# Norm factors put on behind the projections, and half of a recurrence's operands made on another engine

## The chip, the cores and the metric

The kernel runs on one core of a Trainium2 chip. The metric is the device time of one execution in microseconds; before the change the median of three runs is 1512.39 us (1511.13 to 1512.42). A profile of one execution, with every instruction's start and duration, is the basis of all that follows. TensorE (PE) multiplies, VectorE (DVE), ScalarE (ACT) and GpSimd (POOL) work elementwise, and SyncE (SP) issues most of the transfers.

## The reference

Two transformer blocks are computed for 256 tokens of 1024 features in float32. The change touches only the mixer of the first block, which is, cut to what matters:

```python
u = rmsnorm(h, norm1_g)        # h * rsqrt(mean(h*h) + 1e-6) * g, the mean over the features of a token
proj = u @ w_in
p_rwkv, p_att, p_idx, p_gate = split(proj)
y_a = rwkv7_mix(token_shift(p_rwkv, tshift_mu), ...)
q, k = rope(q), rope(k)                      # q, k, v from p_att
y_b = dsa_attention(q, k, v, rope(q_idx), rope(k_idx), w_idx)
g_a, g_b = split(sigmoid(p_gate))
h = h + (g_a * (y_a @ w_o_rwkv) + g_b * (y_b @ w_o_att)) @ w_out
```

`token_shift(p, mu)` is `p + (prev - p) * mu` with `prev` the token before. `rwkv7_mix` is a recurrence over time with a 64 by 64 state per head, decays, and normalised keys. The norm's factor belongs to a token, so it can be put on `u` or on any column of `proj`. Behind the mixer come a gated feed-forward layer, and the second block with its own mixer and a mixture of 64 experts; these are as they were.

## The kernel before

**Layout.** Features lie on partitions, tokens along the free axis: the input `xT` is eight blocks of 128 features by 256 tokens. A projection group is 256 columns of a weight matrix, loaded as one tile `w` of 128 by 2048 (L258), so two slots `w0`, `w1` hold two groups.

**Three products for one.** Each operand is split in a high part (rounded) and a low part (the rest): `wh` by a cast on ScalarE (L272), `wl` by a subtraction on VectorE (L273), in pieces of 128 by 512. These are kept in a ring of three half groups. The activation has `uh` and `ul` in the same way. `dense` (L299) issues, for eight blocks of features and two halves of the columns, the three products high-high, high-low and low-high: 48 products of 128x256 per group. The weight pieces are the product's first operand, so the output has columns on partitions, and a token's factor lies along the free axis.

**The norm.** `Rms` squares the input on ScalarE (L375), adds pairs of blocks on VectorE (L382), sums over partitions with TensorE (`nps`, L390), takes the root on ScalarE (L394) and its reciprocal on VectorE (L395), and `rows` (L406) spreads the 256 factors over all partitions with TensorE (`rsp`). Then `scaled_parts` (L427) multiplies each block by gain and factor on VectorE (L433), casts `uh` on ScalarE (L435) and makes `ul` on VectorE (L436). `hold` keeps the first weight casts behind the root in ScalarE's order. `raw_pair` (L420), which multiplies by the gain alone, is used at the second norm.

**What is done with the groups.** First group 6, whose columns are the low-rank inputs of decay, rate and gate (`lor0`). Then for head group 0 its r, k, v (groups 0, 2, 4), and for head group 1 groups 1, 3, 5; `shift_group` (L466) does the token shift out of PSUM, one scaled copy on ScalarE and one multiply-add on VectorE per 128 columns. `rwkv(g)` (L556) makes the decays (`sg`, `aa`, `cum`, `cpv`: sigmoid, running sum, exponentials), normalises the keys (`kk`, by `kps`, a root, a reciprocal of `kn` and the spreading `bps`), and writes the operands of the chunked recurrence: `zr` with minus-kk times decay (L625) and r times decay (L627), `bh` = `aa` and `kh` = `km` divided by the decay, and `bp`, `kp` (L635, L636, GpSimd), which are transposed (`tps`). Products `mps` give masks `MB`, `MK`; `solve` inverts a triangular system in six levels, with masks made on GpSimd (L497); then four steps of the recurrence run. `dsa_proj` (L778) makes the groups of the attention, with a rotation of q, k and the indexer's by `cos` and `sin`; `gate_steps` (L812) takes a group through tanh on ScalarE; `select` keeps 64 keys per query, by eight rounds of MAX and MATCH_REPLACE on VectorE; `attend` follows.

**What sets the order.** Each engine runs its instructions in one fixed order. The framework's scheduler interleaves the code's chains when the kernel is built, and waits are kept by semaphores; so an instruction that waits holds up all behind it on its engine. Projection groups fill TensorE while the recurrence's short products wait on other engines.

## Time and profile before

| | |
|---|---|
| runs, median | 1512.39 us |
| profiled execution, its own time | 1515.65 us |
| its span | 1513.9 us |
| TensorE busy | 1438.2 us, 95% |
| VectorE busy | 823.9 us, 54% |
| ScalarE busy | 596.1 us, 39% |
| GpSimd busy | 137.0 us, 9% |
| DMA | 362.10 MB, mean 239 GB/s |

The first block's mixer, where the change lies, takes about the first 345 us. A profile's timeline row gives the start, the time, the engine, the source line, the operation with output and inputs, the shape and how many were merged; in brackets stands the idle time of the engine before it and who ended it. PEld is TensorE's weight load. Busy shares over the whole span mix stages with different limits, so the windows and timelines of a stage are what to read.

### The profile page before, as it was taken

To read this page: it belongs to the slowest core of one execution; us is meant where nothing else is said; L and a number is where in the kernel's file an instruction comes from. 1 tells how busy PE (TensorE), PEld (TensorE's weight loads), DVE (VectorE), ACT (ScalarE), POOL (GpSimd) and SP (SyncE) were. 2 spreads that over 40 slices of the span, in tenths; PEclk is the share of its full clock that TensorE was granted. 3 is DMA by queue.
4 is the path that set the end of the run, shared out by engine and by line. 5 is a ranking of instruction groups with operands and counts; after the bars stand their busy time and mean duration, and the time that the engine had idled before them with its cause. 6 is when DMAs were issued, how large, how long until landed. Compare 5 with 4: busy or idle time off the path is not lost. (4 is left out here: it accounts for less than half of the span.)

```text
span 1513.9 us, 28057 instructions
## 1 busy us (share of the span) xinstructions
PE 1438.2 (95%) x11310; PEld 1157.3 (76%) x11310; DVE 823.9 (54%) x1664; ACT 596.1 (39%) x1221; POOL 137.0 (9%) x131
## 2 busy tenths in 40 slices
PE   6999999989999989899999999999999999988996
PEld 6788988989999969798898999996554544543543
DVE  4787488577998968855854567653122121211211
ACT  5543356555545467444534555552111111111110
POOL 2143210000100100310230000100000000000000
PEclk9999999989999989899999999999999999999999
DMA  5311244549978345222321433975999999999996
GB/s 197 123 50 42 67 161 140 184 167 422 389 292 306 125 165 186 84 84 72 124 85 56 168 115 109 347 284 197 352 413 421 423 422 421 422 422 422 421 423 264
DMA packets 58627, 362.10 MB, mean 239 GB/s; under 512 B 6912, under 2 KB 7552, under 8 KB 20352
## 3 DMA queue, kind: packets, MB, share of 16 engines
q1 hardware_dynamic: 56912, 357.77, 60.7%
q10 hardware_dynamic: 1584, 2.52, 0.5%
q8 instruction: 90, 1.47, 0.4%
q14 instruction: 41, 0.34, 0.1%
HBM read 357.51 MB, written 1.05 MB: 237 GB/s over the span
## 5 line engine op out<-in xcount | busy, mean ns | idle before, releaser
L286 PE MATMUL dps<-uh,wh 128*128 128x256 f32 x1280 | 376.2, 294 | 4.2 <-ACT wh L272 2.1
L286 PE MATMUL dps<-uh,wl 128*128 128x256 f32 x1280 | 365.0, 285 | 4.0 <-DVE wl L273 4.0
L286 PE MATMUL dps<-ul,wh 128*128 128x256 f32 x1280 | 365.2, 285 | 0.7 <-DVE ul L439 0.5
L286 PEld LDWEIGHTS dps<-uh,wh 128*128 128x128 f32 x1280 | 244.0, 191 | 15.5 <-issue 8.6
L286 PEld LDWEIGHTS dps<-ul,wh 128*128 128x128 f32 x1280 | 243.6, 190 | 7.0 <-issue 4.3
L286 PEld LDWEIGHTS dps<-uh,wl 128*128 128x128 f32 x1280 | 243.4, 190 | 6.2 <-DVE wl L273 4.8
L273 DVE TENSOR_TENSOR wl<-w,wh 128x512 fp32r<-128x512 f32 x267 | 193.1, 746 | 58.0 <-ACT wh L272 56.4
L286 PE MATMUL gup<-wx,xg 128*32 128x512 f32 (+2 forms) x1016 | 201.8, 600 | 20.7 <-DMA wx<-in_w_exp_dram 20.7
L272 ACT CAST wh<-w 128x512 fp32r<-128x512 f32 x267 | 154.4, 615 | 141.8 <-PE dps L286 100.2
L286 PEld LDWEIGHTS gup<-wx,xg 128*32 128x32 f32 (+2 forms) x1016 | 58.6, 122 | 138.4 <-issue 99.5
L273 DVE TENSOR_TENSOR wl<-wm,wh 128x512 fp32r<-128x512 f32 x200 | 140.3, 732 | 39.6 <-ACT wh L272 39.3
L272 ACT CAST wh<-wm 128x512 fp32r<-128x512 f32 x200 | 115.9, 618 | 111.3 <-PE dps L286 72.7
L1694 DVE COPY cs<-pxt 128x1 f32<-128x1 f32 x27 | 4.3, 158 | 216.0 <-PE pxt L289 216.0
L1720 DVE TENSOR_TENSOR yl<-dnp,yh 128x512 fp32r<-128x512 f32 x54 | 37.3, 691 | 153.4 <-ACT yh L1719 153.4
L286 PE MATMUL dnp<-wx,hT 128*32 128x512 f32 (+1 forms) x528 | 100.2, 596 | 2.1 <-DMA wx<-in_w_exp_dram 1.4
L1700 ACT ACTIVATE sgx<-gup 128x256 f32<-128x256 f32 x27 | 10.4, 384 | 222.0 <-PE gup L286 222.0
L1719 ACT CAST yh<-dnp 128x512 fp32r<-128x512 f32 x54 | 31.6, 585 | 119.6 <-PE dnp L286 119.6
L286 PEld LDWEIGHTS dnp<-wx,hT 128*32 128x32 f32 (+1 forms) x528 | 27.9, 120 | 46.3 <-issue 39.5
L996 DVE SCALAR_TENSOR_TENSOR ada<-wm,ct,ada 128x512 f32<-128x512 f32 x76 | 59.5, 825 | 0.0
L286 PE MATMUL acc<-PT,yh 128*128 128x256 f32 x216 | 55.1, 293 | 0.0
L286 PE MATMUL gat<-P,hth 128*128 128x256 f32 (+1 forms) x224 | 54.8, 287 | 0.0
L286 PE MATMUL acc<-PT,yl 128*128 128x256 f32 x216 | 53.0, 283 | 0.6 <-DVE yl L1720 0.6
(541 smaller groups left out, 2795.3 us busy)
## 6 DMA issues: line engine op xcount, KB each, us to landing
wx<-in_w_exp_dram SPq DMA_DIRECT2D x159, 1024.0 KB, 15.9
w<-in_w_in_dram SPq DMA_DIRECT2D x44, 1024.0 KB, 4.9
wm<-in_w_ada_dram SPq DMA_DIRECT2D x22, 1024.0 KB, 7.8
wm<-in_w_in_dram SPq DMA_DIRECT2D x21, 1024.0 KB, 4.9
wh<-in_w_exp_dram SPq DMA_DIRECT2D x33, 512.0 KB, 15.9
wl<-in_w_exp_dram SPq DMA_DIRECT2D x33, 512.0 KB, 14.7
wm<-in_ffn_in_dram SPq DMA_DIRECT2D x16, 1024.0 KB, 9.2
wm<-in_ffn_out_dram SPq DMA_DIRECT2D x7, 1024.0 KB, 9.3
```

The source lines that it names most:

```text
L272: nc.scalar.copy(hi[:, c:e], x[:, c:e])
L273: nc.vector.tensor_sub(lo[:, c:e], x[:, c:e], hi[:, c:e].bitcast(F32))
L286: latest[0] = nc.tensor.matmul(*args, **kw)
L996: nc.vector.scalar_tensor_tensor(y, x, ct[:, k:k + 1], y, op0=ALU.mult, op1=ALU.add)
L1694: nc.vector.tensor_copy(self.cs, px[:, 256:257])
L1700: nc.scalar.activation(sg, self.pg[:, 0:256], AF.Silu)
L1719: nc.scalar.copy(yh[:, quar(c, 512)], pd)
L1720: nc.vector.tensor_tensor(yl[:, quar(c, 512)], pd, yh[:, quar(c, 512)].bitcast(F32), op=ALU.subtract)
```

## The change

The mixer's projections take the input times the gain only. The factors are computed behind the first group's products: `Rms` gets a list `later`, in which the squares are kept, and `factors()` sums them, takes the root, and writes the factors as a column `rsc` per token tile, as rows `rsr`, and scaled as `rsw`. They are then put on in several ways. `times_rs` multiplies a group's sums in PSUM by `rsr`, in place, on VectorE: for the seven shift groups and the eight gate groups, 15 in all. The rotated groups get it by `cos` and `sin`, which are multiplied once on GpSimd. The values and the index weights, whose tokens lie on partitions, get it as the scale of their copy on ScalarE. `hold` goes. The second part: the r-times-decay operands of `zr` (four instructions per head group) are made on GpSimd instead of VectorE. Nothing else is changed in the code.

```diff
+            if self.later is None:
+                self.sums(0, sq[:, 0, :], g)
+            else:
+                self.later.append((sq[:, 0, :], g))
+
+        def finish(self):
+            self.p = pt("d", "nps")
+            for x, g in self.later:
+                self.sums(0, x, g)
...
-                with tc.issue_after(hold[0]) if hold else nullcontext():
-                    nc.scalar.copy(hi[:, c:e], x[:, c:e])
+                nc.scalar.copy(hi[:, c:e], x[:, c:e])
...
-    norm = Rms(xT, r2(0))
+    norm = Rms(xT, r2(0), None, [])
+    uu = parts()
     for g in range(4):
         norm.pair(g)
-    _, uu, _ = scaled_parts(xT, lambda b: pcol("norm1_g", b), norm.rows(norm.columns()))
-    hold.append(norm.root.ins)
+    def factors():
+        norm.finish()
+        rsc.append(norm.columns())
+        nc.vector.tensor_scalar(rsw, rsc[0], float(64 ** -0.5 * 8 ** -0.5), None, op0=ALU.mult)
+        nc.scalar.copy(rsr, norm.rows(rsc[0]))
+
+    def times_rs(p):
+        p3 = p.rearrange("p (a s) -> p a s", a=2)
+        nc.vector.tensor_tensor(p3, p3, rsr.unsqueeze(1).to_broadcast([128, 2, S]), op=ALU.mult)
+        return p
...
         p = yield from dense(A["w_in"][g], uu)
+        if not rsc:
+            factors()
+        times_rs(p)
...
-    whole(shift_group(6, lor0))
-    hold.clear()
+    steps = shift_group(6, lor0)
+    for g in range(4):
+        raw_pair(uu, xT, lambda b: pcol("norm1_g", b), g)
+        for _ in range(2 if g else 0):
+            next(steps)
+    whole(steps)
...
                 load_consts(rp, 1)
+                for t in ("cos", "sin"):
+                    nc.gpsimd.tensor_tensor(cc(t), cc(t), rsr, op=ALU.mult)
...
-                nc.vector.tensor_tensor(zr[hf, j, :, i, 1, :], ck(r)[hf, j], ck(PP)[hf, j], op=ALU.mult)
+                nc.gpsimd.tensor_tensor(zr[hf, j, :, i, 1, :], ck(r)[hf, j], ck(PP)[hf, j], op=ALU.mult)
...
-            nc.scalar.activation(wi[:, n, :], p[:, 0:8], AF.Copy, scale=float(64 ** -0.5 * 8 ** -0.5))
+            nc.scalar.activation(wi[:, n, :], p[:, 0:8], AF.Copy, scale=rsw[:, n:n + 1])
...
-            nc.scalar.copy(vt[:, :, 256 * i:256 * (i + 1)], p.rearrange("p (n c) -> p n c", n=2))
+            for n in range(2):
+                nc.scalar.activation(vt[:, n, 256 * i:256 * (i + 1)], p[:, 256 * n:256 * (n + 1)], AF.Copy, scale=rsc[0][:, n:n + 1])
...
-        nc.scalar.activation(t, (yield from dense(src, uu)), AF.Tanh, scale=0.5)
+        p = yield from dense(src, uu)
+        nc.scalar.activation(t, times_rs(p) if first else p, AF.Tanh, scale=0.5)
```

Since the scheduler places every instruction anew, the order moves on all engines up to the end of the mixer; behind it, it is the same. Three places matter. A row gives line, operation, output and inputs (tile numbers behind the names where they tell rows apart), shape and count.

First, TensorE at the start. Before, its first rows are:

```order
L286 MATMUL nps<-ones,nsq 128x1 x8
L286 MATMUL rsp<-cst_74,rsc 128x128 x2
L286 MATMUL dps<-uh,wh 128x256
L286 MATMUL dps<-ul,wh 128x256
L286 MATMUL dps<-uh,wh 128x256
```

Now the products of group 6 come first, with five of the eight sums between the second and the third of them; behind its last product stand:

```order
L283 MATMUL dps<-uh,wl 128x256
L283 MATMUL dps<-uh,wh 128x256
L283 MATMUL dps<-ul,wh 128x256
L283 MATMUL dps<-uh,wl 128x256
L283 MATMUL nps<-ones,nsq 128x1 x3
L283 MATMUL rsp<-cst_74,rsc 128x128 x2
L283 MATMUL dps<-uh,wh 128x256
L283 MATMUL dps<-ul,wh 128x256
```

The last sums and the broadcast `rsp` moved from before the first product to behind the 48th, ahead of group 0.

Second, VectorE at the key normalisation of head group 0. Before, from the decay to the reciprocal of `kn` (`wl_1075` is the second half of group 3's weights):

```order
L575 TENSOR_TENSOR cpv_471<-cum_470,sg_453 128x512
L627 TENSOR_TENSOR zr_516<-r_229,cum_470 64x4x64 x4
L473 SCALAR_TENSOR_TENSOR r_232<-dps_998,par_72,r_232 128x255
L607 TENSOR_SCALAR km_502<-aa_454,par_72,oka_143 128x256 x2
L273 TENSOR_TENSOR wl_1075<-w_1066,wh_1074 128x512
L597 TENSOR_SCALAR kn_482<-kn_482 8x256
L609 TENSOR_TENSOR km_502<-km_502,k_230 128x512
L598 RECIPROCAL kn_482<-kn_482 8x256
```

Now, for the same stretch (`dps_999` is group 1's sums, and `wl_1077` are the two last pieces of group 3's weights):

```order
L607 TENSOR_TENSOR cpv_472<-cum_471,sg_454 128x512
L476 TENSOR_TENSOR dps_999<-dps_999,rsr_101 128x512
L639 TENSOR_SCALAR km_503<-aa_455,par_72,oka_105 128x256 x2
L270 TENSOR_TENSOR wl_1077<-w_1068,wh_1076 128x512
L641 TENSOR_TENSOR km_503<-km_503,k_226 128x512
L270 TENSOR_TENSOR wl_1077<-w_1068,wh_1076 128x512
L629 TENSOR_SCALAR kn_483<-kn_483 8x256
L645 SCALAR_TENSOR_TENSOR rk_507<-r_225,par_72,km_503 128x256
L630 RECIPROCAL kn_483<-kn_483 8x256
```

The four `zr` rows are gone, a multiplication of group 1's sums stands in their place, and both pieces of `wl_1077` come before the reciprocal, where before only one did.

Third, TensorE at the transposes behind that. Before, 30 products of groups 3 and 5 lie between the transposes of `v` and the first of `bp`; the end of them and the transposes are:

```order
L286 MATMUL dps_1132<-ul_115,wh_1135 128x256
L286 MATMUL dps_1132<-uh_114,wl_1136 128x256
L286 MATMUL dps_1132<-uh_114,wh_1135 128x256
L286 MATMUL dps_1132<-ul_115,wh_1135 128x256
L286 MATMUL dps_1132<-uh_114,wl_1136 128x256
L286 MATMUL dps_1132<-uh_114,wh_1135 128x256
L289 MATMUL tps_546<-cst0_74,bp_530 128x128
L289 MATMUL tps_550<-cst0_74,kp_531 128x128
```

Now, from the transposes of `v` on (`dps_1135` is group 5, `dps_1747` the indexer's narrow group, `lps` the low-rank products of head group 1):

```order
L286 MATMUL tps_542<-cst0_74,v_227 128x128 x2
L283 MATMUL dps_1135<-uh_87,wh_1138 128x256
L283 MATMUL dps_1135<-ul_88,wh_1138 128x256
L283 MATMUL lps_1206<-lor_213,low0_107 128x512
L283 MATMUL lps_1210<-sgd_214,low1_108 128x256
L283 MATMUL dps_1747<-uh_87,wh_1750 72x256
L283 MATMUL dps_1747<-ul_88,wh_1750 72x256
L286 MATMUL tps_547<-cst0_74,bp_531 128x128
L286 MATMUL tps_551<-cst0_74,kp_532 128x128
L286 MATMUL tps_547<-cst0_74,bp_531 128x128
L286 MATMUL tps_551<-cst0_74,kp_532 128x128
```

Group 3's last products moved ahead of the transposes of `v`, and those of group 5 behind the transposes of `bp` and `kp`.

## Rows read from the trace of the kernel before

**Rows 1.** Windows: start:end, length, busy us of PE, PEld, DVE, ACT, POOL; clock, DMA.

```profile
60.00:70.00 10.00, 7.51 (x35) 6.12 (x34) 9.79 (x20) 1.97 (x6) 3.49 (x5) 0.83 0.11 31
...
330.00:340.00 10.00, 6.36 (x44) 6.21 (x43) 5.76 (x12) 6.54 (x12) 0.00 (x0) 0.79 0.45 152
340.00:350.00 10.00, 10.00 (x77) 10.00 (x76) 3.19 (x5) 4.63 (x8) 0.29 (x1) 0.87 1.01 422
...
220.00:250.00 30.00, 28.37 (x218) 25.72 (x217) 29.18 (x98) 17.38 (x43) 0.00 (x0) 1.00 0.27 94
```

**Rows 2.** Timeline of the first 30 us, several engines.

```profile
2.15 0.91 SPq L258 DMA_DIRECT2D w<-in_w_in_dram  x2
...
7.07 0.17 DVE L459 TENSOR_SCALAR omm<-par 128x14 f32<-128x14 f32 x1 [6.05 <-DMA par<-in_params_dram]
...
7.23 1.42 DVE L382 TENSOR_TENSOR nsq<-nsq 128x256 f32<-128x256 f32 x4
...
11.83 1.22 PE L286 MATMUL rsp<-cst,rsc 128*128 128x128 f32 x4 [0.55 <-DVE rsc L395]
...
19.34 0.58 PE L286 MATMUL dps<-uh,wl 128*128 128x256 f32 x1 [1.40 <-DVE wl L273]
...
24.63 0.41 PE L286 MATMUL dps<-uh,wl 128*128 128x256 f32 x1
...
24.84 0.41 PE L286 MATMUL dps<-uh,wh 128*128 128x256 f32 x1
...
25.24 0.28 PE L286 MATMUL dps<-uh,wl 128*128 128x256 f32 x1
...
25.36 0.28 PE L286 MATMUL dps<-uh,wh 128*128 128x256 f32 x1
...
27.68 0.47 ACT L472 ACTIVATE lor<-dps,omm 128x256 f32<-128x256 f32 x1 [2.31 <-PE dps L286]
```

**Rows 3.** Tile w in the first 14 us: from issue to landing.

```profile
DMA to landing us min/median/max: 7.4/8.6/9.9
```

**Rows 4.** Page, costliest groups: ScalarE's weight casts (count, busy, mean ns).

```profile
L272 ACT CAST wh<-w 128x512 fp32r<-128x512 f32 x267 | 154.4, 615 | 141.8 <-PE dps L286 100.2
```

**Rows 5.** Groups by form, VectorE, 0 to 340 us (busy us, mean ns).

```profile
L425 DVE SCALAR_TENSOR_TENSOR ul<-hT,par,uh 128x256 fp32r<-128x256 f32 x8 | 3.5, 480 | 0.6 <-ACT uh L424 0.6
```

**Rows 6.** Groups by form, VectorE, 340 to 560 us.

```profile
L963 DVE TENSOR_TENSOR silu<-dps,rsf 128x512 f32<-128x512 f32 x11 | 7.6, 687 | 3.2 <-PE dps L286 3.2
```

**Rows 7.** Timeline of VectorE, 27 to 112 us.

```profile
54.10 1.53 DVE L627 TENSOR_TENSOR zr<-r,cum 64x256 f32<-64x256 f32 x4 [3.40 <-ACT cum L582]
...
58.12 1.73 DVE L598 RECIPROCAL kn<-kn 8x256 f32<-8x256 f32 x1
...
66.00 0.68 DVE L630 TENSOR_TENSOR aa<-aa,sg 128x512 f32<-128x512 f32 x1
...
82.16 0.68 DVE L504 TENSOR_TENSOR X<-sps,cst 128x512 f32<-128x512 f32 x1
82.75 1.47 DVE L273 TENSOR_TENSOR wl<-w,wh 128x512 fp32r<-128x512 f32 x1
```

**Rows 8.** Timeline of TensorE, 58 to 76 us.

```profile
63.30 0.44 PE L289 MATMUL tps<-cst,v 128*128 128x128 f32 x2
66.14 0.58 PE L286 MATMUL dps<-uh,wl 128*128 128x256 f32 x1 [2.40 <-DVE wl L273]
...
71.31 0.27 PE L289 MATMUL tps<-cst,bp 128*128 128x128 f32 x1
```

**Rows 9.** Timeline of GpSimd, 27 to 112 us.

```profile
66.83 0.92 POOL L635 TENSOR_TENSOR bp<-aa,PC 128x256 f32<-128x256 f32 x1 [4.47 <-DVE aa L630]
...
69.76 1.06 POOL L636 TENSOR_TENSOR kp<-km,PC 128x256 f32<-128x256 f32 x1
...
82.38 1.30 POOL L497 TENSOR_TENSOR nm<-MB,cst 128x512 f32<-128x512 f32 x1 [0.69 <-DVE XT L505]
```

More of the change, by code (lines that the diff above doesn't have):

```diff
@@ L241, in _body @@
     npart = [0]
-    hold = []
     def more_slots(pool_, n, tag="wm"):
@@ L364, in _body, with __init__ @@
     class Rms:
-        def __init__(self, h, ring, gain=None):
-            self.h, self.ring, self.gain = h, ring, gain
-            self.p = pt("d", "nps")
+        def __init__(self, h, ring, gain=None, later=None):
+            self.h, self.ring, self.gain, self.later = h, ring, gain, later
+            if later is None:
+                self.p = pt("d", "nps")
             nc.scalar.activation(nrm, epsd[:, 0:1], AF.Sqrt)
@@ L382, in pair @@
             nc.vector.tensor_tensor(sq[:, 0, :], sq[:, 0, :], sq[:, 1, :], op=ALU.add)
-            self.sums(0, sq[:, 0, :], g)
+            if self.later is None:
[3 more added lines that the diff above has]
+        def finish(self):
+            self.p = pt("d", "nps")
+            for x, g in self.later:
+                self.sums(0, x, g)
         def sums(self, o, x, g):
@@ L449, in _body @@
     r2 = lambda g: lambda name: rp.tile([128, 2, S], F32, name=name, tag="r2%d" % g, bufs=NR2)
-    norm = Rms(xT, r2(0))
+    norm = Rms(xT, r2(0), None, [])
+    uu = parts()
     for g in range(4):
         norm.pair(g)
-    _, uu, _ = scaled_parts(xT, lambda b: pcol("norm1_g", b), norm.rows(norm.columns()))
-    hold.append(norm.root.ins)
+    rsr = rp.tile([128, S], F32, name="rsr")
+    rsw = rp.tile([128, 2], F32, name="rsw")
+    rsc = []
+    def factors():
[7 more added lines that the diff above has]
+        return p
     omm = rp.tile([128, 14], F32, name="omm")
@@ L806, in dsa_proj, with gate_steps @@
                 yield
-            nc.scalar.copy(vt[:, :, 256 * i:256 * (i + 1)], p.rearrange("p (n c) -> p n c", n=2))
+            for n in range(2):
+                nc.scalar.activation(vt[:, n, 256 * i:256 * (i + 1)], p[:, 256 * n:256 * (n + 1)], AF.Copy, scale=rsc[0][:, n:n + 1])
     ga = ap_.tile([128, NB, S], F32, name="ga", tag="s1", bufs=1)
     gcol = lambda t, g: fl(t[:, 2 * g:2 * g + 2])
-    def gate_steps(t, src):
-        nc.scalar.activation(t, (yield from dense(src, uu)), AF.Tanh, scale=0.5)
+    def gate_steps(t, src, first=False):
+        p = yield from dense(src, uu)
+        nc.scalar.activation(t, times_rs(p) if first else p, AF.Tanh, scale=0.5)
     for g in range(2):
@@ L820, in _body @@
     for g in range(4):
-        fill.add("ga", gate_steps(gcol(ga, g), A["w_in"][15 + g]))
+        fill.add("ga", gate_steps(gcol(ga, g), A["w_in"][15 + g], True))
     bias = dp.tile([128, 2, S], F32, name="bias")
@@ L911, in _body @@
     for g in range(4):
-        gate_group(gcol(gb, g), g, A["w_in"][19 + g])
+        whole(gate_steps(gcol(gb, g), A["w_in"][19 + g], True))
     tap("ya", fl(yA))
```

## Prediction

> **What bounds the kernel now.** I read four views, in this order. First the windows: from 0 to about 345 us, the first block's mixer, TensorE is busy nearly throughout. It is short of work at the start, between 60 and 70 us, where the granted clock also drops (0.83 over the 10 us), and a little between 220 and 250 us, where VectorE is busy for 29.18 of 30 us [rows 1]. So in this stretch the time falls only where a TensorE gap closes, and rises where one opens; what stands behind 345 us is unchanged and just shifts. Second the timeline of the start [rows 2]: the norm's sums, root and row broadcast end at 11.83 + 1.22 = 13.05, then VectorE scales the input, and the even run of products begins only at 19.34, with the first low half of a weight. Products are 0.21 us apart until 25 us (24.63, 24.84) and 0.12 us apart behind (25.24, 25.36): the clock's two levels, 1.2 and 2.4 GHz. Group 6 (the first 48 products, for the low-rank columns) has four issued before 19.34, some 28 at the slow pace and 16 at the fast one: it ends near 27.1, and ScalarE reads it at 27.68. Third, timelines of VectorE, TensorE and GpSimd at the second gap [rows 7 to 9]. Fourth, prices by form [rows 4 to 6].
>
> The sum is made against the profiled execution, 1515.65 us (span 1513.9, so 1.75 around it). That is 3.26 above the median of the three runs, 1512.39; I carry the difference over to the median. About 0.2%, 3 us, is what a measurement can tell from no change.
>
> **Front: products start earlier, a gain.** Root, broadcast and eight scalings leave the way to the first product. ScalarE now makes the high parts straight from the input once the parameters are there, at 7.07, at some 0.45 each (0.47 is a scaled 128x256 form, at 27.68): four by 8.9. The first weights are issued at 2.15 and land 7.4 later, at 9.55 [rows 2, 3]; a cast takes 0.62 [rows 4]: the first at 10.2. VectorE ends the four sums of squares at 7.23 + 1.42 = 8.65, makes four low parts at 0.48 [rows 5], to 10.5, then the first low weight (0.69, nearest form [rows 6]), to 11.2. From there the products run without a hole: each further 12 (2.6 us at the slow pace) need one low weight and two low parts, 1.7 us of VectorE. If the pace rises as long after the even start as before (25.1 - 19.34 = 5.8), it rises at 17.0; by then 29 are done, and 19 at 0.118 end at 19.2.
>
> Here the moved step stands: three sums, root, reciprocal and broadcast now come behind group 6 on TensorE. ScalarE has a weight cast (0.62) ahead of the root, VectorE a low weight (0.69) and the reciprocal (0.2) ahead of the broadcast, so it starts near 20.8 and takes about 0.7 at the full pace, rather more than half of 1.22. Group 0 starts at 21.6 instead of 27.1: **5.5 us gained**. Bounds: 7.0 if the pace rises at 15, 3.8 if the hole of 1.5 us costs a stretch at half clock (1.7, below).
>
> Put at nothing in the front: the third weight load, which waits for a slot, is issued when the first group's low parts are made, near 13, and keeps ahead; the second low-rank load moves some 4 us forward on ScalarE's queue, a quarter of a weight load in size, and could hold the first weights back by 0.3; cos and sin times the factors, two of about 0.65 on GpSimd, run while it has nothing else, and the low-rank copy queued behind them waits longer for its data. The value copies and the index weights scaled on ScalarE lie in its pauses; 0.5 each if those go.
>
> **The key normalisation of head group 0: a loss.** Before, VectorE writes four r-times-decay operands in 1.53 (54.10), ends the reciprocal at 59.85 and the second product of aa at 66.68 [rows 7]; GpSimd's four decayed operands end at 69.76 + 1.06 = 70.82 [rows 9]; TensorE idles for 2.40 before 66.14 [rows 8] and runs at half clock for some 3.4 us (0.83 granted in 10 us [rows 1]), which costs 1.7. Together 4.1 us.
>
> After, in the same coordinates: a multiplication of 0.69 (128x512, PSUM with the factor row [rows 6]; that it writes back to PSUM no row shows, and I take the same) stands in place of the 1.53, and a low weight (0.69) moves ahead of the reciprocal: 59.7. The four operands now run on GpSimd from 54.1 on. 256 elements a partition cost 0.65 as half of the 512 that took 1.30 at 82.38, and 0.92 to 1.06 as its own forms of that size did at 66.83 and 69.76 [rows 9].
>
> Do they stop VectorE as well? At 82.75 a low weight took 1.47 instead of 0.69 and ended 0.54 after GpSimd's operation (82.38 + 1.30 = 83.68), while one with a PSUM input took 0.68 at 82.16, across that operation's start [rows 7, 9]. So VectorE's work on two SBUF tensors waits for GpSimd's. Four times 0.65, less the 0.69 that reads PSUM, is 1.9 at worst; it is 0 if they meet nothing of that kind. I take 1.0: reciprocal at 60.7.
>
> The Trainium skill (SBUF — State Buffer, Who interferes with whom) says that a VectorE instruction with two SBUF inputs contends with a GpSimd instruction that reads SBUF, and that whoever issues first keeps the shared pair for its whole instruction. By that rule this term is the 1.9, and the sum 0.9 later than mine; without it the term is 0 and the sum 1.0 earlier. The 1.47 at 82.75 agrees with it.
>
> From the reciprocal to the end of aa there were 6.8 us, a low weight among them; without it 6.1: aa ends at 66.8, GpSimd's operands near 70. What changes is TensorE's cover. Before, 30 products lie between the transposes of v (63.30) and of bp and kp (71.31 [rows 8]); now, by the order, two products and two low-rank ones, and two narrow products. TensorE, at 63.7 before, has ten products of the group put first and these behind: it stands ready near 65.4, wherever the reciprocal's delay falls, and idles until 70, 4.6 us. Half clock behind the hole costs 1.7 again, or 3.4 if it lasts twice as long, as behind the gap in 330 to 340 us (0.79 and 0.87 in two windows [rows 1]); I take 2.4. That is 7.0 against 4.1: **2.9 us lost**. Bounds: 0.8 (nothing blocked, short stretch) and 5.0 (full blocking, long stretch). The products that no longer fill the hole are still to be done, so its length counts in full.
>
> **Selection: a small loss.** Four gate groups get a multiplication of 0.69 each [rows 6], 2.8 us in VectorE's full stretch; ScalarE took the gates straight from PSUM. Between 0 and 2.8 I take **0.8**, nearer to 0, since TensorE idles for only 1.6 of those 30 us (28.37 busy [rows 1]) and weights are made ahead. The other four gates and the later shift groups lie beside TensorE's products; 0.69 each if these run out. Head group 1's four operands move to GpSimd behind the solver's masks: nothing, or 1.9 lost if they block.
>
> **Sum:** -5.5 + 2.9 + 0.8 = -1.8 us: 1513.85 for the profiled execution, 1510.6 by the median. By the bound above that is no change.
>
> **Rivals.** *The front gain stays.* GpSimd's operands meet VectorE's PSUM work, the reciprocal is early, the hole is no longer than before, the selection hides its part: -5.5 + 0.8 = -4.7, 1507.7. For it: 82.16 shows PSUM work unhindered, and 1.53 leaves VectorE. Against: the order leaves the transposes without cover whatever GpSimd does. 0.38.
>
> *VectorE becomes the bound, slower.* Fifteen multiplications of 0.69 are 10.4 us more on VectorE, against 3.8 of scalings and 3.1 of operands taken away, and the operands still block it. Its place: the two key normalisations and the selection. Price: -5.5 + 5.0 + 1.9 + 2.8 = +4.2, 1516.6. It decides once the three together pass 5.5 + 3 = 8.5. For it: 29.18 of 30 us [rows 1]. Against: only TensorE's idle time counts. 0.17.
>
> *It does not do what it says.* The weights land no earlier, and TensorE could stay at the slow pace until 25 us whatever it does; group 0 would then start near 24.2, the gain is 2.9, the sum +0.8, 1513.2. For it: the rows 0.21 apart until 25. Against: the clock was back some 3.4 us after 66.14 with even work. 0.10, a part of no change.
>
> **How the numbers follow.** My forecast has 0.35 and the third rival 0.10: 0.45 for within 3 us; faster 0.38, slower 0.17. The likeliest case's own range is 1508.5 to 1513.5. The whole range goes from 1505 (front 7.0, key term 0.8, nothing for the selection, 1 us of scatter) to 1516 (nearly the second rival).
>
> **What would show it.** Right: even products from about 11.2, group 0 near 21.6 behind a hole of 1 to 2 us ahead of the broadcast; a TensorE hole of 4 to 6 us ahead of the transposes of bp, waiting for GpSimd, with a clock drop; VectorE rows of 1 us and more while GpSimd writes zr. Wrong: no such hole (faster), a new wait for low weights between 210 and 250 us (slower), or even products later than 13.

## The result, and the profile after

**1522.06 us**, median of four runs (1521.32 to 1524.09), against 1512.41 (1511.13 to 1512.97) for the kernel before, run on the same chip. The ratio of paired runs is 1.0057, with an interval of 1.0038 to 1.0075: 8.6 us slower (5.8 to 11.4); the two medians by themselves lie 9.7 apart. The prediction was 1510.6 in a range of 1505 to 1516, with 0.17 for slower: the sign was wrong and the range missed.

The profiled execution of after took 1521.32, with a span of 1519.5; the spans of the two profiled executions differ by 5.6. The execution of before that was profiled lay 3.2 above its median, so about 3 us of the 8.6 stand in no comparison of the two traces.

Two of the windows of [rows 1], in the kernel after (the columns are those of [rows 1]):

```profile
60.00:70.00 10.00, 6.44 (x30) 4.07 (x30) 7.55 (x13) 3.69 (x11) 3.22 (x4) 0.83 0.01 2
...
220.00:250.00 30.00, 29.19 (x210) 25.73 (x209) 29.66 (x98) 16.94 (x39) 0.00 (x0) 1.00 0.27 89
```

The second gap is still there (6.44 busy of 10, clock 0.83), and the stretch from 220 to 250 us is as full as before: VectorE 29.66, TensorE 29.19. Neither tells where 5.6 us came from. Windows of fixed times seldom do, once the start has moved. So I cut both spans at the same instructions instead: the first product of the low-rank columns (lps, 45.20 before, 40.02 after), the first product with zr in head group 0 (mps, 74.05 and 69.08), head group 1's first product aps behind the solver (170.87 and 172.38), and two weight casts on ScalarE (343.66 and 344.33; 512.84 and 515.74). Windows between these marks, after and then before (same columns):

```profile
40.02:69.08 29.06, 24.31 (x145) 19.05 (x143) 20.70 (x39) 18.25 (x41) 6.40 (x9) 0.95 0.15 47
69.08:172.38 103.30, 101.23 (x920) 89.59 (x919) 67.40 (x130) 36.59 (x84) 44.88 (x41) 1.00 0.18 58
172.38:344.33 171.95, 165.79 (x1398) 155.38 (x1398) 126.16 (x269) 90.55 (x196) 11.48 (x8) 0.98 0.47 157
344.33:515.74 171.41, 170.70 (x1431) 169.66 (x1430) 152.85 (x231) 87.15 (x153) 14.21 (x10) 1.00 0.82 323
```

```profile
45.20:74.05 28.85, 26.23 (x165) 21.76 (x164) 21.58 (x41) 18.10 (x41) 4.30 (x5) 0.94 0.24 78
74.05:170.87 96.82, 95.97 (x904) 86.56 (x903) 71.63 (x130) 36.21 (x84) 40.60 (x37) 1.00 0.19 64
170.87:343.66 172.79, 164.54 (x1392) 153.29 (x1392) 121.16 (x260) 89.73 (x194) 11.51 (x8) 0.97 0.45 152
343.66:512.84 169.18, 168.47 (x1431) 167.43 (x1430) 152.47 (x230) 87.29 (x153) 14.37 (x10) 1.00 0.82 325
```

Read the length, TensorE's busy time and its count of products. At the first mark the kernel after is 5.18 us ahead. From there the stretches cost +0.21, **+6.48** (96.82 to 103.30), -0.84 and **+2.23** (169.18 to 171.41, with the same 1,431 products and the same idle time, 0.71). The work from 515.74 to the end of the span is longer by 2.70 more. Sum: -5.18 + 0.21 + 6.48 - 0.84 + 2.23 + 2.70 = +5.6. So the front's gain came about as forecast, and two things ate it: head group 1's stretch, and a slow drift over code that the change does not touch.

**The drift.** TensorE's weight loads between 345 and 510 us, by form (count, busy us, mean ns, idle before). After, then before:

```profile
L283 PEld LDWEIGHTS dps<-uh,wh 128*128 128x128 f32 x311 | 59.7, 192 | 0.0
...
L283 PEld LDWEIGHTS acc<-acth,wh 128*128 128x128 f32 x144 | 27.1, 188 | 0.0
```

```profile
L286 PEld LDWEIGHTS dps<-uh,wh 128*128 128x128 f32 x317 | 59.5, 188 | 0.0
...
L286 PEld LDWEIGHTS acc<-acth,wh 128*128 128x128 f32 x144 | 27.0, 188 | 0.0
```

In these products the weights are loaded and uh or ul streams past them. Loads of products with uh take 192 ns instead of 188; those of products with acth, another streamed operand in the same stretch, take 188 in both. The starts of products with uh or ul lie 120.0 ns apart after and 117.8 before, of those with acth 117.8 in both. The rows counted here for uh and ul hold 933 products in the trace of after (three forms of 311), and 933 x 2.2 ns is 2.05 of the 2.23 us. Their instructions are the same; by the addresses in the two built programs, one thing about their operands has changed. The high and low parts begin at bytes 54272 and 62464 of each partition, before at 54336 and 62528. Both new ones are multiples of 512, as nearly all starts of the weights are; the old ones lie 64 beyond. The change calls `parts()` ahead of the norm, so the 64 bytes of the norm's factor tile `rsc`, which stood ahead of the parts, now stand behind them.

**Head group 1.** GpSimd after, then VectorE after and before (start, duration, engine, line, operation; in brackets the wait and what ended it):

```profile
48.98 2.92 POOL L659 TENSOR_TENSOR zr<-r,cum 64x256 f32<-64x256 f32 x4 [23.35 <-ACT cum L614]
...
100.46 1.28 POOL L522 TENSOR_TENSOR nm<-MB,cst 128x512 f32<-128x512 f32 x1 [0.44 <-PE sps L283]
...
103.45 3.10 POOL L659 TENSOR_TENSOR zr<-r,cum 64x256 f32<-64x256 f32 x4
```

```profile
49.63 0.70 DVE L476 TENSOR_TENSOR dps<-dps,rsr 128x512 f32<-128x512 f32 x1 [4.10 <-PE dps L283]
51.94 0.73 DVE L639 TENSOR_SCALAR km<-aa,par,oka 128x256 f32<-128x256 f32 x2 [1.61 <-POOL zr L659]
...
97.93 0.69 DVE L607 TENSOR_TENSOR cpv<-cum,sg 128x512 f32<-128x512 f32 x1
...
106.58 0.74 DVE L639 TENSOR_SCALAR km<-aa,par,oka 128x256 f32<-128x256 f32 x2
...
109.63 1.73 DVE L630 RECIPROCAL kn<-kn 8x256 f32<-8x256 f32 x1
```

```profile
90.16 0.69 DVE L575 TENSOR_TENSOR cpv<-cum,sg 128x512 f32<-128x512 f32 x1
...
98.01 1.00 DVE L607 TENSOR_SCALAR km<-aa,par,oka 128x256 f32<-128x256 f32 x1
...
102.66 1.73 DVE L598 RECIPROCAL kn<-kn 8x256 f32<-8x256 f32 x1
```

The changed key km is written at 106.58; before it began at 98.01, although the kernel after was 4.97 ahead at the last mark. km takes a slot of a ring (a few tiles of memory that are used in turn), the one in which the decays (cum) lie: both stand at the same addresses. The last readers of the decays are the r-times-decay operands, which the change put on GpSimd. In head group 0 the row says so: VectorE waited 1.61 for zr. In head group 1 GpSimd makes the operands behind the solver's masks (nm, 100.46), from 103.45 to 106.55, and km follows at 106.58. But there no wait is shown: VectorE was at work for the solver until 106.43, so GpSimd can have held km up by 0.15 at most. Most of the delay is older. The last step of the decays themselves (cpv) comes at 97.93 instead of 90.16, ahead of all of this. The reciprocal comes at 109.63 instead of 102.66, and the transposes of bp behind it, before and after:

```profile
116.57 0.27 PE L289 MATMUL tps<-cst,bp 128*128 128x128 f32 x1
```

```profile
56.79 1.13 PE L283 MATMUL bps<-kn,cst 128*128 128x256 f32 x4 [1.17 <-DVE kn L630]
...
63.32 0.33 PE L286 MATMUL tps<-cst,bp 128*128 128x128 f32 x1 [1.90 <-POOL bp L667]
...
127.28 0.33 PE L286 MATMUL tps<-cst,bp 128*128 128x128 f32 x1 [1.31 <-POOL bp L667]
```

The first bp of head group 1 comes 10.7 us later (127.28 for 116.57), and TensorE idles 1.31 ahead of it.

### The profile page after: what moved, and what is told of

Same layout as the page of the kernel before. It is cut to its first block, busy times and chain, and to the rows that moved or that the text cites. A ratio compares the mean times of both kernels' runs of the same rounds, so it can differ in the third digit from the quotient of the medians.

```text
span 1519.5 us, 28086 instructions
## 1 busy us (share of the span) xinstructions
PE 1445.2 (95%) x11310; PEld 1165.1 (77%) x11310; DVE 822.8 (54%) x1664; ACT 598.3 (39%) x1224; POOL 144.7 (10%) x141
## 5 line engine op out<-in xcount | busy, mean ns | idle before, releaser
L283 PE MATMUL dps<-ul,wh 128*128 128x256 f32 x1280 | 369.4, 289 | 0.7 <-DVE ul L446 0.7
L283 PEld LDWEIGHTS dps<-uh,wh 128*128 128x128 f32 x1280 | 247.1, 193 | 22.0 <-ACT wh L269 10.0
L283 PEld LDWEIGHTS dps<-ul,wh 128*128 128x128 f32 x1280 | 247.2, 193 | 6.7 <-issue 4.3
L283 PEld LDWEIGHTS dps<-uh,wl 128*128 128x128 f32 x1280 | 246.7, 193 | 2.8 <-issue 1.7
L283 PEld LDWEIGHTS dnp<-wx,hT 128*32 128x32 f32 (+1 forms) x528 | 27.9, 120 | 48.9 <-issue 39.6
L283 PE MATMUL gat<-P,htl 128*128 128x256 f32 (+1 forms) x224 | 54.3, 281 | 0.0
```

What stands on the lines that cost most here:

```text
L283: latest[0] = nc.tensor.matmul(*args, **kw)
```

## The experiments

All times are medians with the kernel before run beside them. us values are the ratio's, times 1514. Where a change moves the order of work, it does so on several engines at once, since the scheduler places every instruction anew; the kernels that move the place alone keep the order (with `rsc` first that of the kernel after, the next two that of the kernel before, on every engine).

### Is it the place?

**Undo the place alone.** In the kernel after, `rsc` is taken when the norm object is made, ahead of `parts()`:

```diff
+            else:
+                self.r = ap_.tile([128, 2], F32, name="rsc", tag="rsc", bufs=2)
...
-            r = ap_.tile([128, 2], F32, name="rsc", tag="rsc", bufs=2)
+            r = ap_.tile([128, 2], F32, name="rsc", tag="rsc", bufs=2) if self.later is None else self.r
```

> The changed kernel with one edit: the small tile of the norm's factors is taken from its pool before the two input parts, as in the kernel before, so that the parts lie 64 bytes further on again; every instruction and its order stay. Theory A (place of the input parts): products that read them are back from 120 ns to 117 to 118 ns apart, in 345 to 520 us as before; some 4,000 such products at 2 ns each make 7 to 10 us, so 1512 to 1515 us. Theory B (first block's holes: key normalisations, gate multiplications): nothing moves, 1522 us.

1517.11 (12 runs) against 1513.95; ratio 1.0017 (1.0003 to 1.0031), +2.6. The loads are back at 188:

```profile
L283 PEld LDWEIGHTS dps<-uh,wh 128*128 128x128 f32 x316 | 59.3, 188 | 0.0
```

**Make the place alone**, in the kernel before:

```diff
...
+    u0 = parts()
-    _, uu, _ = scaled_parts(xT, lambda b: pcol("norm1_g", b), norm.rows(norm.columns()))
+    _, uu, _ = scaled_parts(xT, lambda b: pcol("norm1_g", b), norm.rows(norm.columns()), u=u0)
```

> The kernel before with one edit: the two input parts are taken from their pool before the norm's factors, so that they lie 64 bytes earlier, where the changed kernel has them; every instruction and its order stay. Theory A: products that read them go from 117 to 118 ns to 120 ns apart, 7 to 10 us slower than the kernel before: 1519 to 1522 us. Theory B: no change, 1512 us.

1519.19 (12 runs); 1.0030 (1.0018 to 1.0042): **+4.5** (2.7 to 6.4), with the same instructions in the same order on every engine. Spacing 120.0, loads at 192:

```profile
L286 PEld LDWEIGHTS dps<-uh,wh 128*128 128x128 f32 x311 | 59.7, 192 | 0.0
```

So the place is a cause, from both sides. The ratios of the kernel after and of the one with `rsc` first differ by 0.0040, 6 us; the drift in the trace is 2.23 + 2.70 = 4.9.

**Which places?** One kernel puts the parts 128 beyond a multiple of 512 (a 128-byte tile ahead, one of 384 behind):

> The kernel before with the input parts 64 bytes further on than before (128 bytes beyond where the changed kernel has them) and all that lies behind them in SBUF moved by 512 bytes; every instruction and its order stay. Theory A in a first form (what counts is the place modulo 128 bytes against the weights', which start at multiples of 512): 120 ns between products, 1519 to 1522 us. In a second form (only the same place modulo 512 is slow): 117 to 118 ns or less, 1512 us or less. Theory B: no change, 1512 us.

1514.25 (10 runs); 0.9998 (0.9984 to 1.0012). Spacing 118.8 on average, in a mix of 115 to 122: in between, and no loss that can be measured. Three more kernels, for the spacing alone, gave the parts of each stage 512 spare bytes and began each at another offset, `parts(o)`:

> The kernel before; the input parts get tiles with 512 bytes to spare and are placed at other offsets from a multiple of 512 bytes in each stage: 256 in the first block's mixer, 192 in its feed-forward layer, 320 in the second block's mixer, 32 for the experts' input. Order and work stay; so far 0 gave 120.0 ns between products, 64 gave 117.8 (at times 113.4), 128 gave 118.8 on average. Theory A (the spacing hangs on the place modulo some power of two): each stage gets one spacing of its own, between 113 and 120 ns; if 128 bytes is the period, 117.8 for 192 and 320 and 120 for 256. Theory B (the place is not the cause, the state of the pipeline is): spacings mixed within a stage, no order.

> As the run before, with the offsets 32 in the first block's mixer, 384 in its feed-forward layer, 448 in the second block's mixer, 96 for the experts' input. Theory A with a period of 128 bytes: 120 ns for 384, 117.8 for 448, something else for 32. With a period of 512: 384 as 128 (118.8) or something of its own. Theory B: mixed.

> As s1_offsets and s2_offsets, with the offsets 96 in the first block's mixer, 48 in its feed-forward layer, 16 in the second block's mixer, 112 for the experts' input. So far 0 and 256 gave 120.0 ns, 64, 192, 320 and 448 gave 117.8 or 113.4, 128 and 384 a mix of 115 to 122 (118.8 on average), 32 a mix of 113 to 122 (about 117). Theory A: a spacing of its own for each, mixes for those that are no multiple of 64.

Single runs, 1512.59, 1514.65 and 1512.24. Mean spacing in ns by the start modulo 512, these and the kernels above together (two values are two stretches of a run; 0 and 64 were seen in every stage, each of the others in one or two):

```
0: 120.0   256: 119.9
128: 118.8   384: 118.8
64: 117.8, in stretches 113.4   192: 113.4, 117.7   320: 117.6   448: 117.7, 114.5
32: 116.7 to 117.4   48: 118.4   96: 119.9   16: 118.5, 117.5
```

Worst are multiples of 256, and 96; best the odd multiples of 64, and 32. At the odd multiples of 64, two paces stand side by side for the same address: 117.8 and 113.4. What switches between them I didn't find.

In all of these products the weights begin at multiples of 512, so the place could count by itself or against that of the weights. The second block's gathering products (gat) tell: there the parts of the experts' input, in the same slot and so moved by the same 64 bytes, are the weights, and a matrix P streams past them from a multiple of 256 in every kernel. With the weights 64 beyond a multiple of 256 their starts lie 114.3 ns apart (before) and 114.2 (`rsc` first), with the weights at one 118.5 (after) and 118.6 (the place alone). The products of acc with PT and yh or yl, where both operands begin 192 beyond a multiple of 256 in all four kernels, take 119.5 in all four. So it is the place of the streamed operand against that of the weights: slow is where both begin at the same place modulo 256 (and, in the one stage that had it, 96 beyond that). The 448 gathering products at 4.3 ns are 1.9 us of what the place costs.

### Which part of the change costs the rest?

**The operands back on VectorE**, once in the kernel after and once with `rsc` first as well:

```diff
-                nc.gpsimd.tensor_tensor(zr[hf, j, :, i, 1, :], ck(r)[hf, j], ck(PP)[hf, j], op=ALU.mult)
+                nc.vector.tensor_tensor(zr[hf, j, :, i, 1, :], ck(r)[hf, j], ck(PP)[hf, j], op=ALU.mult)
```

> The changed kernel with the r-times-decay operands made on VectorE again; the input parts stay where the changed kernel has them. Theory A: the products stay 120 ns apart; at most the holes ahead of the transposes of bp and kp (4.2 us in both head groups) shrink, 1519 to 1522 us. Theory B: GpSimd's operands are the loss, so most of the 9.7 us comes back: 1512 to 1515 us.

1523.91 (5 runs); 1.0062 (1.0041 to 1.0082), +9.4.

> The changed kernel with the factors' tile taken first and the r-times-decay operands on VectorE: the front and the factors behind the products alone, at the old place in SBUF. If the two parts of the change cost separately (GpSimd alone 12.5 us, both 3.2 us more than the kernel before), the front alone would be 9 us faster, 1504 us. If either part alone already pushes the second head group's preparation behind the first solve, it is slower than before: 1516 to 1520 us.

1518.89 (12 runs); 1.0027 (1.0014 to 1.0040), +4.1. The two differ in the place alone, and by 5.3 us, which is a third measure of it. TensorE in the second one (the first row of bp in head group 0, the second in head group 1), and the stretch of head group 1 between its marks:

```profile
62.77 0.48 PE L286 MATMUL tps<-cst,bp 128*128 128x128 f32 x1 [3.87 <-POOL bp L669]
...
127.75 0.48 PE L286 MATMUL tps<-cst,bp 128*128 128x128 f32 x1 [2.73 <-POOL bp L669]
```

```profile
69.01:176.11 107.10, 102.72 (x929) 91.77 (x928) 70.70 (x136) 38.30 (x88) 42.93 (x37) 0.97 0.16 52
```

Here VectorE, with the new multiplications on top of the operands, is late with bp's inputs in both head groups: holes of 3.87 and 2.73. Head group 1's stretch is longer than in the kernel after (107.10 for 103.30), though no operand of GpSimd stands in its way: cpv comes at 96.66, km at 106.79, the reciprocal at 108.97, as late as in the kernel after. So the new multiplications, with the order that comes with them, are enough to make head group 1 late.

**The operands on GpSimd alone**, in the kernel before: in both head groups, in the first, in the second (`g == 0` and `g == 1`):

```diff
-                nc.vector.tensor_tensor(zr[hf, j, :, i, 1, :], ck(r)[hf, j], ck(PP)[hf, j], op=ALU.mult)
+                (nc.gpsimd if g == 1 else nc.vector).tensor_tensor(zr[hf, j, :, i, 1, :], ck(r)[hf, j], ck(PP)[hf, j], op=ALU.mult)
```

> The kernel before with only the r-times-decay operands made on GpSimd; the input parts stay where they were. If GpSimd's operands lengthen the key normalisations (blocked VectorE, late bp and kp), 1515 to 1517 us, with a wait for bp on TensorE over 2.4 us. If they relieve VectorE there, as the run with them back on VectorE says, 1509 to 1512 us. If they lie beside other work, no change.

> The kernel before with the r-times-decay operands of head group 0 alone on GpSimd. In its order head group 1's preparation stands behind head group 0's solve, as with both groups on GpSimd (g1_decay_alone, 1525.9 us). Theory C: about the same, 1522 to 1527 us. Theory D: half of it, 1518 to 1521 us.

> The kernel before with the r-times-decay operands of head group 1 alone on GpSimd. In its order head group 1's preparation stands among head group 0's solve, as before. Theory C: 1513 to 1516 us. Theory D: 1518 to 1521 us.

1525.94 (6 runs), 1.0078 (1.0063 to 1.0094), **+11.8**; 1523.34 (7 runs), 1.0060, +9.1; 1519.28 (10 runs), 1.0027, +4.1. The two single ones come near the first in sum (13.2), but they aren't prices of the operands alone, since the order of work moves too: with head group 0's operands alone on GpSimd, head group 1's reciprocal comes at 117.88 instead of 102.66, though its own operands stayed on VectorE and its km waited for nothing. In the last kernel the wait is plain. GpSimd, VectorE, TensorE:

```profile
94.71 0.72 POOL L627 TENSOR_TENSOR zr<-r,cum 64x256 f32<-64x256 f32 x1 [1.90 <-ACT cum L582]
95.40 1.26 POOL L497 TENSOR_TENSOR nm<-MB,cst 128x512 f32<-128x512 f32 x1
96.62 2.37 POOL L627 TENSOR_TENSOR zr<-r,cum 64x256 f32<-64x256 f32 x3
```

```profile
99.03 1.45 DVE L607 TENSOR_SCALAR km<-aa,par,oka 128x256 f32<-128x256 f32 x1 [2.09 <-POOL zr L627]
100.40 0.41 DVE L511 COPY T<-sps 128x256 f32<-128x256 f32 x1
```

```profile
100.87 1.10 PE L286 MATMUL sps<-T,XT 128*128 128x64 f32 x8 [1.63 <-DVE T L511]
```

GpSimd makes one operand, then a mask that the solver wanted first, then three more, to 98.99. VectorE stands 2.09 for km, and behind km stands the solver's copy T, which has nothing to do with the keys: TensorE waits 1.63 for it.

But the prices don't simply add over the parts of the change. With the new multiplications there, moving the operands is no loss (1.0027 with them on VectorE, 1.0017 on GpSimd), and without them it costs 11.8. Both alternatives leave VectorE late; what made it late differs, and no run here takes it apart.

**The gates' factor.** With `rsc` first, the eight multiplications of the gates by the norm's row are left out (their values come out without the norm):

```diff
-        nc.scalar.activation(t, times_rs(p) if first else p, AF.Tanh, scale=0.5)
+        nc.scalar.activation(t, p, AF.Tanh, scale=0.5)
```

> The changed kernel with the factors' tile taken first (as in e1_rsc_first, 1517.1 us) and the eight multiplications of the gate groups by the norm's factor left out, so that the gates are taken without the factor. If the selection stage pays for them, 1514 to 1516 us; if they lie beside other work, 1517 us and the loss left in e1 is in the key normalisations alone.

1520.0 (1513.85 to 1522.76, 4 runs); 1.0047 (1.0029 to 1.0065): leaving work out gained nothing that shows in so wide a scatter. It gives no sign that these eight multiplications are dear; the order of work moved here too.

### Is it the wait for the slot?

A rival: head group 1 is late because its preparation stands behind head group 0's solver in the program, whatever the slots do. Then taking the two head groups' code in turn (with `rsc` first) gets it back:

```diff
+    heads = [rwkv(g, yA[:, 2 * g:2 * g + 2]) for g in range(2)]
+    some = lambda g, n: [next(heads[g], None) for _ in range(n)]
+    whole(rkv_proj(0))
+    some(0, 11)
+    whole(rkv_proj(1))
+    some(1, 2)
+    for _ in range(5):
+        some(0, 2)
+        some(1, 1)
...
```

> The changed kernel with the factors' tile taken first (e1_rsc_first, 1517.1 us), and the code of the two head groups written in turn, so that head group 1's low-rank products, key normalisation and transposes stand again among the products of head group 0's solve on TensorE, as in the kernel before, and not behind it. Theory C (the rest of the loss is this late preparation): the front's gain comes through, 1509 to 1513 us. Theory D (GpSimd's operands and the multiplications themselves cost it, wherever they stand): 1517 us as e1.

1516.47 (12 runs) against 1514.44; 1.0013 (0.9998 to 1.0029). That is no different from the kernel that it changes (1.0017). It does bring head group 1 forward, its reciprocal from 109.50 to 98.59, but now VectorE stands for GpSimd's operands ahead of km:

```profile
93.71 1.80 DVE L641 TENSOR_SCALAR km<-aa,par,oka 128x256 f32<-128x256 f32 x2 [4.16 <-POOL zr L661]
```

So this run by itself doesn't tell lateness from the wait. The last run of this part, which has the turns without the wait, does.

**A slot of its own for km**, first where only head group 1's operands are on GpSimd:

```diff
-        km = ring("km")
+        km = rp.tile([128, 2, S], F32, name="km", tag="km%d" % g, bufs=1) if g == 1 else ring("km")
```

> As i2_decay_head1 (the kernel before with head group 1's r-times-decay operands on GpSimd, 1519.3 us), with a slot of its own for head group 1's km. In i2 km takes the slot of the ring that the decays cum leave, whose last readers are these operands, so VectorE stands 2.09 us for GpSimd at 99 us, and the solve's copy T behind it makes TensorE wait 1.63 us. If this reuse is what the move costs, 1514 to 1516 us and no wait of VectorE for zr; if it is GpSimd's time itself (the solver's masks behind the operands, blocked VectorE), 1518 to 1520 us.

1515.51 (12 runs) against 1513.8; 1.0015 (0.9999 to 1.0031), +2.3 instead of +4.1. The two intervals overlap, so the gain isn't shown by the times; but the wait of 2.09 is gone from the trace. What is left there is another thing, GpSimd and then VectorE:

```profile
96.93 2.69 POOL L497 TENSOR_TENSOR nm<-MB,cst 128x512 f32<-128x512 f32 x2
```

```profile
97.08 1.40 DVE L613 SCALAR_TENSOR_TENSOR rk<-r,par,km 128x256 f32<-128x256 f32 x1
...
98.74 1.43 DVE L631 TENSOR_TENSOR km<-km,sg 128x512 f32<-128x512 f32 x1
```

Two VectorE operations on SBUF tensors take 1.40 and 1.43, beside a GpSimd mask; the same forms take 0.47 and 0.68 elsewhere in these traces. This is what the Trainium skill says (SBUF — State Buffer, Who interferes with whom): an operation of VectorE with two SBUF inputs and one of GpSimd that reads SBUF contend for a shared read interface. The trace agrees, with some 0.9 and 0.75 us lost here.

Then with the whole change, `rsc` first, and one tile for both head groups:

```diff
-        km = ring("km")
+        km = rp.tile([128, 2, S], F32, name="km", tag="km", bufs=1)
```

> The changed kernel with the factors' tile taken first (e1_rsc_first, 1517.1 us) and a slot of its own for km (one for both head groups). In the changed kernel VectorE stands 1.61 us for zr ahead of km at 52 us. If the reuse of the slot lengthens the key normalisations, the wait of 1.18 us for kn and part of the 3.3 us for bp and kp go: 1512 to 1515 us. If not, 1517 us.

**1511.75** (1510.16 to 1514.94, 12 runs); 0.9986 (0.9973 to 0.9998): **-2.1 us** (-4.1 to -0.3), faster than the kernel after and, by little, than the one before. Windows between the first four marks, the stretch of head group 1 in the kernel that it changes (`rsc` first), and VectorE's km and reciprocal of head group 1:

```profile
38.71:68.36 29.65, 25.68 (x158) 21.04 (x156) 23.93 (x42) 18.80 (x42) 7.69 (x9) 0.92 0.25 79
68.36:168.05 99.69, 98.09 (x901) 86.93 (x900) 68.78 (x125) 35.58 (x82) 44.50 (x41) 0.99 0.16 51
168.05:340.51 172.46, 164.72 (x1403) 154.26 (x1403) 126.84 (x270) 91.70 (x199) 12.01 (x8) 0.98 0.48 159
```

```profile
68.24:173.60 105.36, 103.26 (x919) 91.13 (x918) 67.42 (x130) 36.60 (x84) 44.89 (x41) 0.97 0.18 57
```

```profile
89.75 0.40 DVE L641 TENSOR_SCALAR km<-aa,par,oka 128x256 f32<-128x256 f32 x1
...
107.09 1.73 DVE L632 RECIPROCAL kn<-kn 8x256 f32<-8x256 f32 x1
```

Head group 1's stretch takes 99.69 instead of 105.36. Not all of that is gained: 18 products fewer lie in it (901 for 919, some 2.2 us), and the third stretch is longer (172.46 for 170.69). The three stretches together take 301.80, with `rsc` first 305.87, before 298.46. km begins at 89.75, long ahead of GpSimd's operands. The reciprocal, though, comes only some 2.5 us earlier (107.09 for 109.50): the kernel's order of work changes with the slot, and how much of the gain is the wait and how much the order, these runs do not separate.

With the wait gone, VectorE meets GpSimd's operands in head group 0, and both are drawn out: the four operands take 3.76 instead of 2.92, and a low weight beside them 1.22, where one takes 0.68 elsewhere:

```profile
48.16 3.76 POOL L661 TENSOR_TENSOR zr<-r,cum 64x256 f32<-64x256 f32 x4 [23.54 <-ACT cum L616]
```

```profile
50.10 1.22 DVE L270 TENSOR_TENSOR wl<-w,wh 128x512 fp32r<-128x512 f32 x1
```

Adding the head groups' code in turn to it:

> As l2_own_km, with the two head groups written in turn as in k1_overlap (1516.5 us). If both costs are real and separate, the lowest of the changed kernels: 1509 to 1513 us, faster than the kernel before. If neither counts, 1516 to 1517 us.

1512.74 (12 runs); 0.9988 (0.9974 to 1.0003), no better, though the reciprocal of head group 1 comes at 95.95 instead of 107.09. Four kernels with `rsc` first make a square: with the ring's slot 1.0017 in the old order of code and 1.0013 with the head groups in turn, with a slot of its own 0.9986 and 0.9988. The slot brings 0.0031 and 0.0025 (4.7 and 3.8 us), the turns nothing in either row. So being late is not in itself what costs, and the rival at the head of this part is out. Left untested is what a slot of its own would bring to the kernel before.

### Other ways to the front's gain

Only group 6 takes the unscaled input, in zr's space; all else reads scaled parts as before, so nothing needs a factor behind its products:

```diff
-        p = yield from dense(A["w_in"][g], uu)
+        p = yield from dense(A["w_in"][g], raw if g == 6 else uu)
...
```

> A third way to the early start: only group 6 takes the input without the factors, from parts of its own in the space of zr, with one multiplication by the factors behind its products; all other groups take scaled parts as in the kernel before, made while group 6 runs, and stand at the same place in SBUF; nothing else changes, and behind the front TensorE's order is that of the kernel before. If the loss of the changed kernel comes from the place of the parts and from the multiplications and order behind the front, this keeps the front's gain: first products at 13 us instead of 19.3, 3 to 5 us faster than the kernel before, 1508 to 1511 us. If VectorE's 16 further operations in the front eat it, 1513 us.

1513.07 (12 runs) against 1514.76; 0.9993 (0.9977 to 1.0009): no difference. Group 6 ends 3.4 us earlier, but VectorE now makes both kinds of low parts, and TensorE waits for the first low weight behind them:

```profile
27.05 0.39 PE L286 MATMUL dps<-uh,wl 128*128 128x256 f32 x1 [2.12 <-DVE wl L273]
```

Behind that hole TensorE runs at half clock from 27.9 to 31.3, and at the first mark the kernel is level with the one before (45.18 for 45.20).

The same with the scaling on GpSimd, and the head groups in turn:

> As v1_raw_group6 (group 6 alone from the input without factors; 1513.1 us, its TensorE short of low weights at 25 us), with the input times the factors made on GpSimd for the other groups, in place of eight operations of VectorE, and the two head groups written in turn as in k1_overlap. If VectorE's work between 24 and 45 us ate the front's gain in v1, this frees 3.4 us of it: 1508 to 1512 us, faster than both kernels. If GpSimd's multiplications come too late or block VectorE, 1513 us or more.

1528.2 (6 runs); 1.0091 (1.0070 to 1.0113): slower, and I have not followed why.

## Why the prediction was wrong

**The front was right.** TensorE after, at the start:

```profile
9.95 0.58 PE L283 MATMUL dps<-uh,wh 128*128 128x256 f32 x1 [9.95 <-ACT wh L269]
...
10.55 2.13 PE L283 MATMUL nps<-ones,nsq 128*128 128x1 f32 x10
12.54 0.56 PE L283 MATMUL dps<-uh,wl 128*128 128x256 f32 x1
...
18.23 0.32 PE L283 MATMUL dps<-ul,wh 128*128 128x256 f32 x1
...
22.21 0.71 PE L283 MATMUL rsp<-cst,rsc 128*128 128x128 f32 x4 [0.83 <-DVE rsc L402]
22.67 0.36 PE L283 MATMUL dps<-uh,wh 128*128 128x256 f32 x1
```

The first product at 9.95, the even run from 12.54 (11.2 forecast; five of the norm's own narrow sums, nps, stood between, 2.13 us from 10.55 on, which the forecast left out though the order showed them), the pace up at 18.23 (17.0), the broadcast at 22.21 behind a hole of 0.83, group 0 at 22.67 (21.6): 4.4 gained there against 27.1, and 5.18 at the first mark. The term was -5.5.

**The key normalisation of head group 0 was about right, though it shows only later.** The holes ahead of bps (1.17) and of the first bp (1.90) came, with two of 0.69 and one of 0.24 between bp and kp: 4.7 us, where 4.6 was forecast. That they agree is in part chance: the forecast was one hole ahead of the transposes that ends with GpSimd, and of that kind are 3.5, while the 1.17 ends with the reciprocal. Half clock lasted 2.99 us behind them, 1.5 lost where 2.4 was taken. Yet the stretch is longer by only 0.21. The reason is in the counts of its windows: 145 products instead of 165. Some 20 products, 2.4 us at 0.12 each, were put off past the mark, and 16 more are in the next stretch (920 for 904). So 0.21 + 20 x 0.12 = 2.6 of the 2.9 forecast. (The term's bounds, printed as 0.8 and 5.0, come out of its own numbers as 1.2 and 4.8.) What stood in it for blocked VectorE work was wrong in kind for this kernel. While GpSimd wrote zr (48.98 to 51.90) no VectorE row was drawn out (the multiplication at 49.63, which works on PSUM, took 0.70): VectorE did not meet GpSimd's operations, it waited for them (1.61). Where that wait was taken away, above, the blocking that was forecast came.

**The step that failed first: head group 1's operands "behind the solver's masks: nothing, or 1.9 lost if they block".** With it the whole stretch was put at nothing. I priced the operands by what they would do to VectorE's SBUF work, and never asked who next takes the memory that they read, nor what the new multiplications and the new order do to head group 1. The stretch lost 6.48; less the 16 products, 1.9, that is 4.6 where I put 0, and 1.2 of it is more idle time of TensorE (2.07 for 0.85). Two things are shown in place of the 0. The slot counts: one of its own for km is worth 4.7 and 3.8 us in two orders of the code. And the multiplications with their order make head group 1 late by themselves: with the operands on VectorE, where no such wait can be, its stretch is 107.10. How much of the slot's gain is the wait (1.61 in head group 0, at most 0.15 in head group 1) and how much the order that comes with it is not separated, and what else makes up the 4.6 stays open.

**The step that failed second: "what stands behind 345 us is unchanged and just shifts".** Its instructions are unchanged, its operands' addresses are not. It cost 4.9 us in the traces and 4.5 to 6 in the runs, shown from both sides. None of the rows read from the kernel before prices it; that the tile had moved stood in the code.

**The rivals.** "VectorE becomes the bound" (1516.6) named the right place, the two key normalisations. With `rsc` first and the operands on VectorE it is what happens in kind, with holes of 3.87 and 2.73 for bp; that +4.1 lies so near to +4.2 is chance, since the selection, 2.8 of the latter, was no part of it: its stretch got 0.84 shorter. In the kernel after, the place cost the larger half, and the rest is open between the late VectorE and the slot. "It does not do what it says" is out: the pace rose at 18.23.

With the place put right and a slot of its own for km, the change is worth -2.1 (-4.1 to -0.3). My sum was -1.8. That the two are so near says little for the terms. Head group 1's stretch is then still 2.9 us longer than before (99.69 for 96.82), the front gained more (first mark at 38.71, after 40.02), and the kernel before was never given that slot.

## What to carry to other kernels

Where a step moves to another engine, list the memory that it is the last reader of, and who takes that slot next: that next writer may now wait there for the slower engine, and everything queued behind it. And where a diff makes a tile earlier or later, compare the addresses of all large operands before and after, also against the weights that they are multiplied with, as one compares instructions: 64 bytes cost nearly as much here (4.5 us) as the earlier start brought (5.2).

## What the runs showed of the hardware

In these runs the distance between TensorE products (256 columns past weights of 128 by 128) hangs on where in its partition the streamed operand begins, against the place where the weights begin. With the weights at multiples of 512 bytes, at full clock and with nothing waiting, it was 120.0 ns with the streamed operand at multiples of 256, 118.8 at 128 beyond, and between 113.4 and 117.8 at odd multiples of 64. With the streamed operand at a multiple of 256 and the weights moved instead, it was 118.5 with the weights at a multiple of 256 and 114.3 at 64 beyond. With both 192 beyond it was 119.5. The loads of the weights take 192 ns and 188 with the streamed operand moved, though the weights stay where they were. Between 120.0 and 117.8 lie 2%, between 120.0 and 113.4 lie 6%. Over this program, 64 bytes cost 4.5 us of 1514 (2.7 to 6.4). Why the place matters, and what lets a stretch run at 113.4, is open.
